# A decoder layer's input projection: eight block products against seven, and a new order of emission

## The chip, the cores and the metric

The kernel runs on one core of a Trainium2 chip. The metric is device time in microseconds (us); less is better. PE is the matmul engine, DVE the vector engine, ACT the activation engine, POOL the GpSimd engine, and SP the queue that issues the DMAs. Each engine works through its own instructions in the order in which the program emitted them, and an instruction that waits holds up all that stands behind it on its engine.

## What is computed

One layer over 2048 tokens of width 1024: a normalised input goes through one projection, its columns feed a gated delta-rule group (8 heads of 128) and a short gated convolution (8 groups of 128), and the two are mixed by an output projection.

```python
h = rmsnorm(x, norm_in_w)
proj = h @ w_in                       # 1024 x (8192 + 16) columns
qkv, z_g, b_g, a_g, gate_b, gate_c, h_c, z_c = split(proj)
qkv = silu(causal_depthwise_conv(qkv, conv_qkv_w))
...
o = gated_delta_rule_chunked(q, k, v, g, beta)     # state S carried from chunk to chunk
o = rmsnorm(o, gdn_norm_w) * silu(z_g)
y_c = gate_b * (causal_depthwise_conv(gate_c * h_c, conv_w) + conv_b) * silu(z_c)
out = rmsnorm(x + concat(o, y_c) @ w_out, final_norm_w)
```

## The kernel before

**Tiling.** The tokens are worked in two halves of 1024, each in two blocks of 512. The projection's columns are 64 tiles of 128, and one narrow tile for the gates. For each tile and block, `dense` (L449) makes one sum of products over the eight 128-row slices of the width. Operands are float32 split in two float16 parts, so each slice takes three matmuls of 512 columns (high by high, low by high, high by low): 24 for a tile and block, all on line L462. A weight tile is read anew in each half.

**Getting a weight tile ready.** `norm_w` (L376) sums the tile's squares on ACT (L383), reduces them over partitions by a small matmul (L386) and makes a power-of-two scale by a short chain over DVE and POOL (L138 to L141, L389, L390); it does so once for a column, in the first half. `split` (L408) makes the high part on ACT (L414) and the low part on DVE (L424).

**One head.** After its k, q and v tiles, `gdn` (L655) multiplies k by k and q (L706, `NA` on DVE at L710), sends the 32x32 diagonal blocks out by DMA, and `invert` (L869) inverts them on POOL by 60 instructions on 32 partitions (L876, L878). The inverses come back by DMA into `Wt`. DVE transposes them at L758, and the first small matmul that needs them is L767. Eight chunks follow, each a chain: L811 (state by k, PE), L812 (`r`, DVE), L817 (PE), L819 (`u`, ACT), L822 (PE), L826 (the state `S_all`, DVE). Matmuls of the dense tiles stand between its steps.

**What sets the order.** Every step is a generator that counts in slots; `slot` (L217) lets each that is due emit its next piece, and `dense` calls it after every eight matmuls. The plan of tiles and the constants at the head of the file (SHIFT, PACE, XL and others) were set by hand. Waits in a generator are numbers of slots.

**The output projection** (L1182 to L1184) is 1536 matmuls of 512 columns. `out_start` (L1085) loads the first weights and the first two mixed rows (`mr`, then `mm` by `split_mix`, L1024) while the last dense tiles are still running.

## Time and profile before

| | |
|---|---|
| median of 3 runs | 2199.77 us (2198.93 to 2204.18) |
| the profiled execution | 2200.84 us, of it 2199.0 us in the span that the profile shows |
| PE busy | 2088.5 us, 95% of the span |
| DVE, ACT, POOL busy | 1177.0, 747.4 and 788.7 us (54%, 34%, 36%) |
| mean granted PE clock | 0.974 of full speed |

Busy time is the share of the span in which an engine had an instruction running. PE's records overlap (a matmul's record is longer than the time to the next one), so its rate is read from the starts of matmuls that follow each other. Where an engine idles, the profile names the instruction that ended the idle time.

### The profile page before, as it was taken

To read this page: it belongs to the slowest core of one execution; us is meant where nothing else is said; L and a number is where in the kernel's file an instruction comes from. 1 tells how busy PE (TensorE), PEld (TensorE's weight loads), DVE (VectorE), ACT (ScalarE), POOL (GpSimd) and SP (SyncE) were. 2 spreads that over 40 slices of the span, in tenths; PEclk is the share of its full clock that TensorE was granted. 3 is DMA by queue.
4 is the path that set the end of the run, shared out by engine and by line. 5 is a ranking of instruction groups with operands and counts; after the bars stand their busy time and mean duration, and the time that the engine had idled before them with its cause. 6 is when DMAs were issued, how large, how long until landed. Compare 5 with 4: busy or idle time off the path is not lost.

```text
span 2199.0 us, 29850 instructions
## 1 busy us (share of the span) xinstructions
PE 2088.5 (95%) x11663; PEld 1252.0 (57%) x11663; DVE 1177.0 (54%) x2153; ACT 747.4 (34%) x1415; POOL 788.7 (36%) x1158
## 2 busy tenths in 40 slices
PE   5999999999999999899899998999899899999998
PEld 3445564645454545465456454555556456888886
DVE  4645566656555555567455455466456435224433
ACT  5524242525242424344224243232323123223221
POOL 2063526253535353605642536526262600000100
PEclk9999999999999999899999998999999999999999
DMA  4342223334653232333332233544434218334452
GB/s 118 59 72 47 70 58 72 54 75 51 77 55 72 48 80 51 116 59 72 49 73 62 64 59 65 46 80 68 53 67 67 64 39 277 125 115 153 162 173 87
DMA packets 235828, 178.98 MB, mean 81 GB/s; under 512 B 43677, under 2 KB 207910, under 8 KB 235686
## 3 DMA queue, kind: packets, MB, share of 16 engines
q1 hardware_dynamic: 235686, 177.06, 37.3%
q8 instruction: 92, 1.51, 0.3%
q14 instruction: 50, 0.41, 0.1%
HBM read 147.53 MB, written 29.49 MB: 81 GB/s over the span
## 4 chain that ended last, share of the span: by engine, by line
PE 62%; POOL 21%; DVE 6%; issue 5%; DMA 4%; ACT 1%; SPq 0%; POOLq 0%; DVEq 0%; ACTq 0%
PE ps_d L462 35%; POOL nb L878 9%; POOL nbt L876 8%; PE ps_d L1182 3%; PE ps_d L1184 3%; PE ps_r L1182 3%; PE ps_d L1183 3%; PE ps_r L1184 3%; PE ps_r L1183 3%; PE ps_t L706 2%; POOL oss L852 2%; DMA E<-gd 2%; PE ps_r L817 1%; PE ps_r L822 1%; DVE cacc L554 1%
## 5 line engine op out<-in xcount | busy, mean ns | idle before, releaser
L462 PE MATMUL ps_d<-hx,wh 128*128 128x512 f16 x4160 | 1284.7, 385 | 2.1 <-DVE hx L307 1.2
L462 PE MATMUL ps_d<-hx,wl 128*128 128x512 f16 x2048 | 789.0, 385 | 5.0 <-DVE craw L573 3.0
L462 PEld LDWEIGHTS <-wh 128*128 128x128 f16 x4160 | 411.9, 100 | 432.8 <-issue 27.1
L462 PEld LDWEIGHTS <-wl 128*128 128x128 f16 x2048 | 209.1, 102 | 220.1 <-issue 14.6
L876 POOL TENSOR_TENSOR nbt<-nb 32x30 f32<-32x30 f32 (+14 forms) x480 | 279.1, 581 | 121.7 <-DMA nb<-nd 88.0
L878 POOL TENSOR_TENSOR nb<-nb,nbt 32x30 f32<-32x30 f32 (+14 forms) x480 | 296.8, 618 | 37.6
L852 POOL TENSOR_TENSOR oss<-oss,nhalf_pow 128x16 f32<-128x16 f32 x32 | 102.2, 3195 | 268.7 <-DVE oss L851 255.4
L414 ACT ACTIVATE wh<-raw,wscale 128x1024 f16<-128x1024 f32 x130 | 148.7, 1144 | 141.3 <-DVE wscale L141 114.1
L554 DVE SCALAR_TENSOR_TENSOR cacc<-craw,cols_a,cacc 128x1024 f32<-128x1024 f32 x144 | 187.4, 1301 | 0.9
L424 DVE SCALAR_TENSOR_TENSOR wl<-raw,wscale,wh 128x1024 f16<-128x1024 f32 x128 | 172.8, 1350 | 19.3 <-ACT wh L414 18.9
L139 POOL TENSOR_TENSOR p<-p,nhalf_pow 128x1 f32<-128x1 f32 x66 | 36.0, 546 | 341.5 <-DVE p L138 341.5
L826 DVE SCALAR_TENSOR_TENSOR S_all<-S_all,dec,ps_r 128x128 f32<-128x128 f32 x120 | 41.5, 346 | 211.3 <-PE ps_r L822 211.3
L1072 POOL TENSOR_TENSOR stat<-stat,nhalf_pow 128x1 f32<-128x1 f32 x16 | 15.3, 957 | 353.5 <-DVE stat L1071 353.5
L577 ACT ACTIVATE craw<-ps_d,wscale 128x512 f32<-128x512 f32 x96 | 65.9, 686 | 200.1 <-PE ps_d L462 200.0
L1030 DVE TENSOR_TENSOR mm<-mr,mm 128x1024 fp32r<-128x1024 f32 x64 | 77.2, 1224 | 89.9 <-ACT mm L1028 89.9
L1182 PE MATMUL ps_d<-wo,mm 128*128 128x512 f32 x256 | 102.4, 400 | 0.1
L1182 PE MATMUL ps_r<-wo,mm 128*128 128x512 f32 x256 | 102.1, 399 | 0.0
L1184 PE MATMUL ps_d<-wo,mm 128*128 128x512 f32 x256 | 100.9, 394 | 0.0
L1184 PE MATMUL ps_r<-wo,mm 128*128 128x512 f32 x256 | 100.9, 394 | 0.0
L1183 PE MATMUL ps_d<-wo,mm 128*128 128x512 f32 x256 | 100.6, 393 | 0.1
L819 ACT ACTIVATE u<-ps_r 128x128 f32<-128x128 f32 x128 | 35.0, 273 | 193.4 <-PE ps_r L817 193.2
L1183 PE MATMUL ps_r<-wo,mm 128*128 128x512 f32 x256 | 100.4, 392 | 0.0
(228 smaller groups left out, 2628.8 us busy)
## 6 DMA issues: line engine op xcount, KB each, us to landing
raw<-in_w_in_dram SPq DMA_DIRECT2D x128, 512.0 KB, 8.0
mr<-mixd SPq DMA_DIRECT2D x64, 512.0 KB, 5.0
E<-gd SPq DMA_DIRECT2D x16, 512.0 KB, 9.3
qs<-gd SPq DMA_DIRECT2D x16, 512.0 KB, 4.2
mixd<-yy SPq DMA_DIRECT2D x16, 512.0 KB, 9.0
mixd<-zs SPq DMA_DIRECT2D x32, 256.0 KB, 2.6
wor<-in_w_out_dram SPq DMA_DIRECT2D x16, 512.0 KB, 5.6
x<-in_x_dram SPq DMA_DIRECT2D x8, 512.0 KB, 5.5
```

The source lines that it names most:

```text
L414: ACT.activation(wh, raw, AF.Copy, scale=s_)
L424: DVE.scalar_tensor_tensor(wl, raw, s_, wh, op0=ALU.mult, op1=ALU.subtract)
L462: PE.matmul(ps[:, 0:BLK], w_[:, k, :], x_[k, b], start=n == 0, stop=n == len(mm) - 1)
L554: DVE.scalar_tensor_tensor(acc, raw[:, j:j + HALF], wq(j, t), acc, op0=ALU.mult, op1=ALU.add)
L577: ACT.activation(raw[0][:, 3 + b * BLK:3 + (b + 1) * BLK], ps, AF.Copy, scale=inv)
L852: POOL.tensor_tensor(oss, oss, nhalf_pow[:, 0:1].to_broadcast([P, nq]), op=ALU.pow)
L876: POOL.tensor_tensor(tv, nb[:, 0:m, m:m + 1].to_broadcast([npart, m, n]), nb[:, m:m + 1, m + 1:32].to_broadcast([npart, m, n]), op=ALU.mult)
L878: POOL.tensor_tensor(nb[:, 0:m, m + 1:32], nb[:, 0:m, m + 1:32], tv, op=ALU.subtract)
L1030: DVE.tensor_tensor(mm[:, 1], mr, mm[:, 0], op=ALU.subtract)
L1182: PE.matmul(ps, mm[:, 0, kk, :], wh, start=k == 0, stop=False)
L1183: PE.matmul(ps, mm[:, 0, kk, :], wl, start=False, stop=False)
L1184: PE.matmul(ps, mm[:, 1, kk, :], wh, start=False, stop=k == KM - 1)
```

## The change

The weight tiles are taken in pairs (k with q, v with z, and the two pairs of the convolution). A pair's two tiles, cut into the two halves of the width, and the two token blocks of a half make a 2x2 by 2x2 product, done by one Strassen level in Winograd's form: seven block products of 4 slices for eight. Each product is 12 matmuls of 512 columns (`product`), so a pair takes 84 instead of 96. The gates' tile is not paired and has 80 matmuls in all instead of 64.

For this, `prepare` makes sums of weight blocks (`st`, `A21`, `A12`) and splits seven operands in float16 (tiles `g1` to `g4`, 3.5 tiles' worth a pair); the x blocks are made into seven operands too (`xop`). Those of the second half are made ahead, stored in DRAM (`x1d`) and loaded by `reload_x` when the first half no longer needs the buffers. Four of the products accumulate in one PSUM bank that ACT copies out four times (`chain`), the other three are added by DVE from banks of their own, with two sums of 512 columns between (`sums`); the products' scale is applied later. `either` gives some sums to POOL. The z gate goes through DRAM (`zd`).

The order of emission comes from clocks: `Clock` keeps an estimated time for each engine and for each tile's readiness, with costs written into the code, and `do` emits an instruction when its inputs are ready by these clocks within 0.3 us and its engine's clock is at most 1.2 us (or `back`) ahead of PE's. The matmuls of the projection are emitted two at a time between rounds of all generators. The loads for the output projection and its first splits are spawned after the last product.

```diff
-SHIFT = (0, 3, 5)
-PACE = 1.75
-XL = (3, 3)
-PAIR = (1,0)
-END = (0,1)
-WS = 4
-NG = (2, 2)
-TG = 2
-WBEG = 2
+BACK = 1.2
+PEQ, DRAIN, SEM = 0.43, 0.2, 0.06
...
+    def cost(self, eng, op, outs, ins, a, k):
...
+        if eng == "POOL":
+            if k.get("op") == ALU.pow:
+                return 0.45 + 0.185 * n
+            if op == "tensor_tensor":
+                return 0.2 + 0.0026 * n
+            return 0.2 + 0.0012 * n
...
-    def slot():
-        clock[0] += 1
-        for t in list(tasks):
-            if t[0] <= clock[0]:
-                try:
-                    t[0] = clock[0] + next(t[1])
-                except StopIteration:
-                    tasks.remove(t)
-
...
+    def do(fn, *a, back=BACK, lead=0.3, **k):
+        e = fn.eng
+        while True:
+            t = clk.ready(e, a, k)
+            cur, q = now(), clk.t[e]
+            late = t > max(cur, q) + lead
+            if not late and q <= cur + back:
+                break
+            yield max(t - lead if late else 0.0, q - back, cur + 0.02)
+        fn(*a, **k)
...
+    def either(n=512):
+        return POOL if max(now(), clk.t["POOL"]) + 0.2 + 0.0026 * n <= \
+            max(now(), clk.t["DVE"]) + 1.0 + 0.001 * n else DVE
...
-            scales[cols[i][0]] = s_, inv
-            ss = sm.tile([P, 1], F32, tag="wss", name="wss")
-            junk = hp.tile([P, KD * P], mybir.dt.bfloat16, tag="r7", name="junk")
-            ACT.activation(junk, raws[i].rearrange("p k c -> p (k c)"), AF.Square, accum_out=ss)
-            yield 3
-            pt = ps_t()
-            PE.matmul(pt[:, 0:1], ones, ss, start=True, stop=True)
-            pow2_below(s_, pt[:, 0:1], 8192.0)
-            yield 1
-            DVE.reciprocal(inv, s_)
...
-            ACT.activation(wh, raw, AF.Copy, scale=s_)
...
-                DVE.scalar_tensor_tensor(wl, raw, s_, wh, op0=ALU.mult, op1=ALU.subtract)
...
+    def reload_x():
+        yield from need(("x1d",))
+        for o in PRODUCTS:
+            yield from need(("free", o))
+            xop[o] = hp.tile([P, KT, 2, BLK], F16, tag=f"X{o}", name="xop")
+            yield from do(SP.dma_start, xop[o].rearrange("p k s w -> p (k s w)"), x1d[o])
+            for kt in range(KT):
+                mark("x1", o, kt)
...
+            yield from do(ACT.activation, g1[:, 0], r1, AF.Copy, scale=s1)
+            st = wst.tile([P, 2, KT, P], F32, tag="st", name="st")
+            A11, A12, A21, A22 = r1[:, 0:KT], r1[:, KT:KD], r2[:, 0:KT], r2[:, KT:KD]
+            yield from do(DVE.scalar_tensor_tensor, g1[:, 1], r1, s1, g1[:, 0],
+                          op0=ALU.mult, op1=ALU.subtract)
+            yield from do(DVE.scalar_tensor_tensor, st[:, 1], A21, rho, A11,
+                          op0=ALU.mult, op1=ALU.subtract)
+            yield from do(either().tensor_tensor, A21, A21, A22, op=ALU.add)
+            yield from do(DVE.scalar_tensor_tensor, st[:, 0], A21, rho, A11,
+                          op0=ALU.mult, op1=ALU.subtract)
+            g2 = wst.tile([P, 2, 2, KT, P], F16, tag="G2", name="g2", bufs=2)
+            yield from do(ACT.activation, g2[:, 0], st, AF.Copy, scale=s1)
+            yield from do(either().tensor_tensor, A12, A12, st[:, 0], op=ALU.subtract)
+            yield from do(DVE.scalar_tensor_tensor, g2[:, 1], st, s1, g2[:, 0],
+                          op0=ALU.mult, op1=ALU.subtract)
+            g4 = wst.tile([P, 2, KT, P], F16, tag="G4", name="g4", bufs=1)
+            yield from do(ACT.activation, g4[:, 0], A12, AF.Copy, scale=s1)
+            yield from do(DVE.scalar_tensor_tensor, g4[:, 1], A12, s1, g4[:, 0],
+                          op0=ALU.mult, op1=ALU.subtract)
+            g3 = wst.tile([P, 2, KD, P], F16, tag="G3", name="g3", bufs=1)
+            yield from do(ACT.activation, g3[:, 0], r2, AF.Copy, scale=s2)
+            yield from do(DVE.scalar_tensor_tensor, g3[:, 1], r2, s2, g3[:, 0],
+                          op0=ALU.mult, op1=ALU.subtract)
...
-        for k in range(KD):
-            mm += [(wh, k, xh), (wh, k, xl)] + ([(wl, k, xh)] if wl is not None else [])
-        for n, (w_, k, x_) in enumerate(mm):
-            while (k, b) not in xh:
-                slot()
-            PE.matmul(ps[:, 0:BLK], w_[:, k, :], x_[k, b], start=n == 0, stop=n == len(mm) - 1)
-            if n % 8 == 7 and n + 1 < len(mm):
-                slot()
-        if fr:
...
+    def product(ps, p, half, j, start, stop=True):
+        o = PRODUCTS[j]
+        wait_for(("w", p, {0: 0, 1: 0, 2: 2, 6: 2, 3: 3, 4: 4, 5: 4}[j]))
+        w = ops.pop((p, j))
+        tag = "x1" if half else "x"
+        for kt in range(KT):
+            wait_for((tag, o, kt))
+            for a, b in ((0, 0), (0, 1), (1, 0)):
+                mm(ps, w(kt, a), xop[o][:, kt, b], start=start and kt == 0 and a + b == 0,
+                   stop=stop and kt == KT - 1 and a == 1,
+                   skip_group_check=not j % 2)
+        run()
...
+        def chain(y):
+            yield from need((p, 0))
+            yield from do(ACT.activation, p1, y, AF.Copy, back=9.0)
...
+        def sums(d):
+            yield from need((p, 1))
+            yield from do(DVE.tensor_tensor, p1, d[1], p1, op=ALU.add, back=9.0)
+            yield from need((p, "y4"))
+            yield from do(either().tensor_tensor, u2, u2, u4, op=ALU.subtract, back=9.0)
+            yield from do(DVE.tensor_tensor, u4, d[3], u4, op=ALU.add, back=9.0)
+            yield from need((p, "y6"))
+            yield from do(either().tensor_tensor, u2, u2, o2[:, BLK:], op=ALU.add, back=9.0)
+            yield from do(DVE.tensor_tensor, u2, d[5], u2, op=ALU.add, back=9.0)
...
+    def out_start():
+        yield from need(*[("post", 2 * H - 1, b) for b in range(2)], *[("mixc", 1, g) for g in range(G)])
+        spawn(load_mix(), 1)
+        spawn(split_mix(), 1)
...
+    mark("quads")
+    spawn(load_wo(), 1)
+    spawn(split_wo(), 1)
+    spawn(load_res(), 2)
+    spawn(load_fnw(), 2)
+    spawn(out_start(), 1)
```

On PE, the chain of one chunk among the projection's matmuls, from the state's matmul (`ps_r<-S_all,kq`) on. Before, from the middle of the first half:

```order
L811 MATMUL ps_r<-S_all,kq 128x128
L814 MATMUL po<-qs,S_all 128x128
L462 LDWEIGHTS wh
L462 MATMUL ps_d<-hx,wh 128x512
L462 LDWEIGHTS wl
L462 MATMUL ps_d<-hx,wl 128x512
L462 LDWEIGHTS wh
L462 MATMUL ps_d<-hx,wh 128x512
L462 LDWEIGHTS wh
L462 MATMUL ps_d<-hx,wh 128x512
L462 LDWEIGHTS wl
L462 MATMUL ps_d<-hx,wl 128x512
```

Three more dense matmuls stand behind these before the chain's next step, so there are eight. Now, the same place of a chunk in the first half (all instructions of the engines have the line L183, the recording wrapper):

```order
L183 MATMUL ps_r<-S_all,kq 128x128
L183 MATMUL ps_o<-kq,S_all 128x128
L183 LDWEIGHTS g_2266
L183 MATMUL ps_d<-xop,g_2266 128x512
L183 LDWEIGHTS g_2266
L183 MATMUL ps_d<-xop,g_2266 128x512
L183 MATMUL ps_r<-r,Wt_164 128x128
L183 LDWEIGHTS g_2266
L183 MATMUL ps_d<-xop,g_2266 128x512
L183 LDWEIGHTS g_2266
L183 MATMUL ps_d<-xop,g_2266 128x512
L183 MATMUL ps_r<-u,kst 128x128
```

Two matmuls stand now where eight stood, at each step of the chain.

On DVE, a stretch of the second half in which dense tiles run beside a head's work. Before:

```order
L424 SCALAR_TENSOR_TENSOR wl<-raw,wscale,wh 128x1024
L738 TENSOR_REDUCE qss<-vp 128x32
L861 SCALAR_TENSOR_TENSOR zs<-on,cols_b,zs 128x512
L748 TENSOR_TENSOR vp<-ps_t,rn 128x512
L843 STREAM_TRANSPOSE on<-osq 128x512
L845 TENSOR_REDUCE op<-on 128x16
L846 SCALAR_TENSOR_TENSOR op<-qss,op 128x16
L748 TENSOR_TENSOR vp<-ps_t,rn 128x512
L752 TENSOR_TENSOR qs<-qs,kq 128x1024
L851 TENSOR_SCALAR oss<-ps_t 128x16
L967 TENSOR_TENSOR yy<-yy,zc 128x1024
L424 SCALAR_TENSOR_TENSOR wl<-raw,wscale,wh 128x1024
```

Now (`g` and `st` are weight operands, `c` the projection's results, `raw` the weights):

```order
L183 SCALAR_TENSOR_TENSOR g_9906<-raw,wsc,g_9906 128x1024
L183 SCALAR_TENSOR_TENSOR st<-raw,wsc 128x512
L183 TENSOR_TENSOR oc<-oc,osq 128x512
L183 SCALAR_TENSOR_TENSOR zb<-oc,cols_b,zb 128x512
L183 SCALAR_TENSOR_TENSOR vacc<-c_9450,wq,vacc 128x1024
L183 SCALAR_TENSOR_TENSOR st<-raw,wsc 128x512
L183 TENSOR_TENSOR raw<-raw,st 128x512
L183 TENSOR_TENSOR c_9812<-c_9812,c_9811 128x512
L183 TENSOR_TENSOR c_9811<-ps_d,c_9811 128x512
L183 STREAM_TRANSPOSE on<-osq 128x512
L183 SCALAR_TENSOR_TENSOR g_9973<-st,wsc,g_9973 128x1024
L183 SCALAR_TENSOR_TENSOR g_10003<-raw,wsc,g_10003 128x512
```

Between a head's own instructions stand now several of the weights' preparation and of the results' sums, most of them with two inputs in SBUF, where one `wl` stood.

On SP's queue, the passage from the projection to the output projection (`wor` are its weights, `mr` the mixed rows, `res` and `xo` the residual, `mixd<-yy` or `mixd<-c` a finished convolution group). Before:

```order
L405 DMA raw<-in_w_in_dram 128x8x128 x3
L969 DMA mixd<-yy 128x8x128
L995 DMA wor<-in_w_out_dram 128x2x512 x2
L1021 DMA mr<-mixd 128x1024 x4
L864 DMA mixd<-zs 128x4x128
L1021 DMA mr<-mixd 128x1024 x2
L995 DMA wor<-in_w_out_dram 128x2x512 x4
L1054 DMA res<-in_x_dram 128x512 x2
L1021 DMA mr<-mixd 128x1024
```

Now:

```order
L183 DMA mixd<-zb 128x4x128
L183 DMA wor<-in_w_out_dram 128x2x512 x3
L183 DMA res<-in_x_dram 128x512 x16
L183 DMA xo<-in_x_dram 128x512 x4
L183 DMA fnw<-in_final_norm_w_dram 128x1024
L183 DMA wor<-in_w_out_dram 128x2x512 x3
L183 DMA mixd<-c_15325 128x8x128
L183 DMA mr<-mixd 128x1024
L183 DMA wor<-in_w_out_dram 128x2x512 x3
L183 DMA mr<-mixd 128x1024 x5
```

The first load of mixed rows stood right behind the first weights; it stands now behind all residual loads and behind the last group's store.

## Rows read from the trace of the kernel before

**Rows 1.** The page's head and part 1: busy time, share of the span, instructions.

```profile
span 2199.0 us, 29850 instructions
PE 2088.5 (95%) x11663; PEld 1252.0 (57%) x11663; DVE 1177.0 (54%) x2153; ACT 747.4 (34%) x1415; POOL 788.7 (36%) x1158
```

**Rows 2.** Windows: stretch, then busy us of each engine, granted clock, DMA share, GB/s.

```profile
0.00:27.30 27.30, 8.41 (x43) 7.24 (x44) 14.81 (x40) 15.58 (x25) 8.81 (x26) 0.92 0.72 211
27.30:1820.00 1792.70, 1708.69 (x10030) 951.46 (x10031) 1013.57 (x1916) 628.45 (x1230) 761.67 (x1115) 0.97 0.35 64
1820.00:2199.00 379.00, 371.41 (x1593) 293.33 (x1591) 148.63 (x198) 103.41 (x162) 18.20 (x17) 0.99 0.46 155
```

**Rows 3.** Chain that ended last, one piece: start, length, engine, line, count.

```profile
359.15 10.38 PE ps_d L462 x48
```

**Rows 4.** Groups by line on PE: count, then busy us, mean ns of one.

```profile
L462 PE MATMUL ps_d<-hx,wh 128*128 128x512 f16 x4160 | 1284.7, 385 | 2.1 <-DVE hx L307 1.2 <-ACT hx L306 0.8
L462 PE MATMUL ps_d<-hx,wl 128*128 128x512 f16 x2048 | 789.0, 385 | 5.0 <-DVE craw L573 3.0 <-DVE wl L424 2.0
```

**Rows 5.** Groups by line and form on DVE and ACT, columns as in Rows 4.

```profile
L424 DVE SCALAR_TENSOR_TENSOR wl<-raw,wscale,wh 128x1024 f16<-128x1024 f32 x128 | 172.8, 1350 | 19.3 <-ACT wh L414 18.9
L1060 DVE TENSOR_TENSOR res<-ps_d,res 128x512 f32<-128x512 f32 x8 | 5.5, 689 | 20.2 <-PE ps_d L1184 20.2
L1076 DVE SCALAR_TENSOR_TENSOR res<-res,stat,fnw 128x512 f32<-128x512 f32 x16 | 12.0, 750 | 4.4 <-POOL stat L1072 4.4
L414 ACT ACTIVATE wh<-raw,wscale 128x1024 f16<-128x1024 f32 x130 | 148.7, 1144 | 141.3 <-DVE wscale L141 114.1 <-PE ps_d L462 21.4 <-DMA mixd<-zs 5.6
L1011 ACT ACTIVATE wo<-wor 128x512 fp32r<-128x512 f32 x32 | 18.9, 622 | 21.9 <-PE ps_r L1184 18.2 <-DMA wor<-in_w_out_dram 3.8
```

**Rows 6.** Windows over three heads' inversions on POOL, columns as in Rows 2.

```profile
429.40:471.70 42.30, 39.25 (x189) 19.35 (x188) 24.63 (x44) 10.68 (x16) 37.91 (x65) 0.96 0.25 49
1014.40:1065.90 51.50, 49.47 (x235) 24.41 (x233) 38.91 (x45) 19.79 (x41) 46.89 (x62) 1.00 0.30 66
1080.10:1116.90 36.80, 36.80 (x218) 21.77 (x217) 10.17 (x18) 7.88 (x14) 32.12 (x61) 1.00 0.22 58
```

**Rows 7.** Timeline of POOL in the second of them: start, us, instruction.

```profile
1020.78 0.50 POOL L878 TENSOR_TENSOR nb<-nb,nbt 32x168 f32<-32x168 f32 x1
...
1024.98 1.50 POOL L878 TENSOR_TENSOR nb<-nb,nbt 32x198 f32<-32x198 f32 x1
```

**Rows 8.** Timeline of DVE, ahead of that inversion and in it.

```profile
1008.97 1.28 DVE L424 SCALAR_TENSOR_TENSOR wl<-raw,wscale,wh 128x1024 f16<-128x1024 f32 x1
...
1022.89 1.58 DVE L424 SCALAR_TENSOR_TENSOR wl<-raw,wscale,wh 128x1024 f16<-128x1024 f32 x1
```

**Rows 9.** Waits of PE: who, for whom, us in total, times, longest.

```profile
PE ps_t L767 <- DVE Vt L758: 27.9, 8, 5.6
PE ps_r L822 <- ACT u L819: 1.6, 3, 0.7
```

**Rows 10.** Timeline of all engines at one step of a chain.

```profile
1809.49 0.38 PE L817 MATMUL ps_r<-r,Wt 128*128 128x128 f32 x2
1809.70 0.69 ACT L650 ACTIVATE zs<-ps_d,wscale 128x512 f32<-128x512 f32 x1 [5.43 <-PE ps_d L462]
1810.28 0.27 ACT L819 ACTIVATE u<-ps_r 128x128 f32<-128x128 f32 x1
...
1810.60 0.49 PE L822 MATMUL ps_r<-u,kst 128*128 128x128 f32 x2 [0.72 <-ACT u L819]
```

**Rows 11.** Timeline of ACT at the start: the first weights' squares, the first result's evacuation.

```profile
13.51 1.06 ACT L383 ACTIVATE junk<-raw 128x1024 bf16<-128x1024 f32 x1 [2.11 <-DMA raw<-in_w_in_dram]
...
34.00 0.69 ACT L577 ACTIVATE craw<-ps_d,wscale 128x512 f32<-128x512 f32 x1 [0.28 <-PE ps_d L462]
```

**Rows 12.** DMA issues: KB each, median us from issue to landing.

```profile
mr<-mixd SPq DMA_DIRECT2D x64, 512.0 KB, 5.0
...
mixd<-yy SPq DMA_DIRECT2D x16, 512.0 KB, 9.0
```

1886 lines of the change are left out of this document (1047 added, 839 removed).

## The prediction, made before the change was run

> **What bounds the kernel now.** The page comes first: PE is busy for 2088.5 of 2199.0 us, the other engines for 34 to 54% [rows 1]. Busy PE alone proves little, since its records overlap, so the second view is the windows by stage. The start up to the first dense matmul takes 27.3 us. The projection with the heads' work in it takes 1792.7 us, and PE is busy for 1708.7 of them, so 84 us are idle. The output projection takes 379.0 us with PE busy for 371.4 [rows 2]. Third, the rate: in the chain that ended last, 48 dense matmuls take 10.38 us, which is 0.2163 us each, with nothing between them [rows 3]. The 4160 and 2048 matmuls of L462 [rows 4] at this rate are 1343 us, three quarters of the middle stage. PE's longest waits are for the inverted blocks that DVE transposes, 28 us in 8 waits, and the chain's steps cost next to nothing: 1.6 us at L822 [rows 9]. So the kernel is bound by PE's work. Every matmul taken away is time, as long as nothing else becomes late.
>
> The profiled execution took 2200.84 us, 1.84 more than its span and 1.07 more than the median. The sum is made against it, and 1 us is taken off at the end.
>
> **What is removed.** The 6208 dense matmuls become 64 pairs x 7 products x 12, and 80 for the gates: 5456. That is 752 fewer, at 0.2163 us: -162.7 us [rows 3, 4]. Their shape stays 128x512 and each still brings its own weight load, so I take the rate as it is. 33 tiny matmuls of the scales go too; they are left out. The output projection keeps its 1536 matmuls.
>
> **What DVE and ACT get for it.** A pair cost DVE two low parts, 2 x 1.35 us [rows 5]. Now it has three splits of the same size (4.05), one of half (0.75), two weight sums at 0.75, three additions from PSUM at 0.69 (2.07), and of four more sums about 1.7 on DVE (107 of them in the order, at 0.69: 1.15): 9.5 us [rows 5]. Over 64 pairs that is 608 against 173 us, so +435 us. In the middle stage DVE was busy for 1013.6 us [rows 2]; it will be for some 1450 of about 1700 us, 85%. ACT also grows, by four evacuations and 3.5 splits a pair, but it starts at 628 of 1793 us [rows 2] and stays well below DVE. DVE's 435 us lie beside PE's work, so by themselves they cost nothing. What they do to the instructions that PE waits for is the next two terms.
>
> **The inversion on POOL.** A head's inverse is made by 60 POOL instructions. Three windows over whole inversions show what DVE does to them. With DVE busy for 10.17 of 36.8 us the inversion takes 36.8 us, with 24.63 of 42.3 it takes 42.3, with 38.91 of 51.5 it takes 51.5 [rows 6]. Inside the last, a subtraction of 168 elements takes 0.50 us while DVE is on other work, and one of 198 takes 1.50 us beside DVE's two-input instructions [rows 7]. DVE pays less: the same split takes 1.28 us ahead of the inversion and 1.58 us in it [rows 8]. From 58% to 76% of DVE is 9.2 us, so at 85% I estimate 56 us, 14 above the usual 42. By the order, one to five of the new sums of 128x512 (three on average) fall in an inversion on POOL as well; at 0.50 x 512/168 = 1.5 us each I count 5 us. So the inverse comes some 20 us later (14 + 5) after the head's own products. PE's order leaves no more room for it than before: between the last product of k and q and the first use of the inverse stand 230 dense matmuls on average, where 229 stood, and before they were just short of enough (28 us of waits in all [rows 9]).
>
> Not all of the 20 us is lost. DVE stands too once it reaches the transposes, and then POOL goes on at the pace of the 36.8 us window: 17 of the 20 us after PE's own delays become 11. PE's further waits in that stretch, of which the next term is one, use up about half. I take 5.5 us for each of 16 heads, 88 us, less the 28 of before: **+60 us**. The ends are -28 (the order happens to fit everywhere) and +180 (13 a head).
>
> **The chain.** Eight dense matmuls stood between a chain's steps; now the commonest number between L817 and L822 is two (67 of 128), so 0.22 us of the step itself and 0.43 of dense work. The row shows 1.11 us from one start to the other, when ACT had to finish another evacuation first (it ended at 1810.39 and `u` started at 1810.28, so part of it was ACT's) [rows 10]. Of 128 such steps 102 stand closer than 1.11 us; what is short adds up to 37 us, and 20 us for the two steps through DVE. With 0.85 us as the price when ACT is free it would be some 20 us in all. I take **+30 us**, nearer to the lower end since ACT stays half idle.
>
> **The start.** ACT finished nothing of the first tile before 34.0 us [rows 11], and the first product here needs no more than that. But the third product needs x blocks that are made from both token blocks. By the order, ACT has 21 splits and copies of 128x512 at 0.62 us, 6 scaled evacuations at 0.69 and 7 instructions on weights (about 1.1 each) to do between the first evacuation and the third product's, 25 us [rows 5, 11], while PE has some 15 us of work. Against the old start, which also idled, that is **+18 us** (10 to 30).
>
> **The passage to the output projection.** Before, the mixed rows were loaded while dense tiles still ran. Now the last group is stored after the last product's sums, its silu and its product (about 5 us by the rows of such instructions); the store lands in 9.0 us, the load behind it in 5.0 [rows 12], and ACT and DVE split it. The first load needs only the heads' part, so it need not wait for the store to land, but it stands behind 21 loads on SP's queue. I take **+22 us** (14 to 30, the upper end with everything in series).
>
> **What the new order gives back.** PE's 84 idle us of before [rows 2] held more than the 28 above: waits at places where a number of slots was too short. An order by readiness should lose less there; I take **-20 us** (0 to -40).
>
> **The sum.** 2200.8 - 162.7 + 60 + 30 + 18 + 22 - 20 = 2148; less 1 for the median, 2147 us, 2.4% faster.
>
> **The rivals.**
> *The order absorbs it (2072 us).* If the clocks' costs are right for POOL under load, the inverse comes when PE gets to it. Then the first term is nothing, the chain 20, the start 15 and the passage 18: 2200.8 - 162.7 + 20 + 15 + 18 - 20 = 2071. For it speaks that the cost in the code, 0.2 + 0.0026 n us, adds up to 38 us for an inversion, near the time at DVE's old load. Against it: DVE's load is no longer the old one [rows 6].
> *POOL starves behind DVE (2245 us, slower).* The mechanism is that of rows 7, with its place at the transposes ahead of the first use of the inverse. If nearly every POOL instruction there waits out a DVE instruction, as 1.50 for 0.50 us shows [rows 7], 60 of them take 80 us or more; PE then waits 11 us or more a head, 180 in all or 150 more than before, and the chain's end through DVE goes to 45: 2200.8 - 162.7 + 150 + 45 + 18 + 22 - 20 = 2253, some 2245 if the start is at its lower end. It decides from about 9 us a head: there the gain is gone. The Trainium skill (SBUF — State Buffer, "Who interferes with whom") says of this that a DVE instruction with two SBUF inputs and a GpSimd instruction that reads SBUF exclude each other, the later one fully blocked. By that rule both would be serial wherever both have work, and this rival would be the forecast. The trace agrees for POOL (1.50 for 0.50 us) but shows DVE held for only 0.3 us of 1.28 [rows 7, 8].
> *It does less than it says (about 2200 us).* With the terms at their middle and 3 us a head more on the inversion's path (48 us) the sum is 2195, within 0.3% of before: the matmuls go, and the same time comes back as waits of PE.
>
> **How the numbers follow.** Forecast's neighbourhood (2100 to 2190): 0.48. Absorbed, below 2100: 0.24. About the same: 0.06. Starved: 0.22. A measurement of this kernel can tell about 0.3%, some 7 us. So faster 0.72, same 0.06, slower 0.22. The range is 2068 to 2245: it takes in the first rival's value and the second's, and leaves about 2 in 10 outside.
>
> **What would show it.** L183's matmuls on `xop` must number 5376 and 80, at 0.216 us when dense. In the middle stage DVE should be busy for 80 to 90% and PE idle for 150 to 250 us. Waits of PE for `Vt` (DVE) near 90 us confirm the inversion's term, near 0 or above 200 the rivals; an inversion should last some 50 to 60 us. Waits for `u`, `r` and `S_all` should add up to 20 to 50 us. PE should stand still for about 20 us ahead of the first `wo` matmul. I am wrong if DVE is idle in much of the middle stage while PE waits for something else, such as the weights' operands or x blocks that come back from DRAM at the half's change.

## The result: 20% slower, and the profile of the changed kernel

The changed kernel takes 2644.95 us (median of 4 runs, 2640.95 to 2648.69), the kernel before 2200.41 on the same chip: a ratio of 1.2017 (95% interval 1.199 to 1.2043). The forecast was 2147 us, at most 2245.

The head of the changed kernel's page and its part 1, which answer to [rows 1]:

```profile
span 2645.9 us, 29590 instructions
PE 2121.5 (80%) x10847; PEld 1238.5 (47%) x10847; DVE 1710.7 (65%) x2669; ACT 996.4 (38%) x1764; POOL 1179.7 (45%) x1283
```

The windows by stage, columns as in [rows 2]: the start, the projection with the heads, the passage, the output projection:

```profile
0.00:29.90 29.90, 6.98 (x24) 4.39 (x25) 13.31 (x43) 16.21 (x28) 10.12 (x26) 1.00 0.74 198
29.90:2187.00 2157.10, 1726.63 (x9287) 933.01 (x9288) 1551.24 (x2434) 876.32 (x1575) 1152.43 (x1240) 0.88 0.40 68
2187.00:2209.00 22.00, 0.42 (x3) 0.02 (x1) 11.06 (x15) 9.36 (x15) 2.69 (x1) 0.59 1.05 385
2209.00:2645.90 436.90, 387.48 (x1536) 301.08 (x1536) 135.13 (x180) 94.53 (x147) 14.50 (x16) 0.93 0.34 112
```

These rows hold the whole account. Behind the start, PE was busy for 1708.69 + 371.41 = 2080.1 us before [rows 2] and is now for 1726.63 + 0.42 + 387.48 = 2114.5: 34 us more, although the dense matmuls that are gone were 163 us of work. So the work that is left takes 197 us longer; the granted clock of the middle stage fell from 0.97 to 0.88. As an estimate, PE's busy time in windows of 2 us, each times what its clock lacked of full speed, adds up to 45 us before and 195 now, so the clock makes some 150 of the 197 us; the rest was not taken apart. PE stands still for 430.5 + 21.6 + 49.4 = 501.5 us, where it was 84.0 + 7.6 = 91.6: 410 us more. With 2.6 us at the start, 197 - 163 + 410 + 3 is the 447 us by which the span grew.

PE's waits in the changed kernel: for whom, us in total, times, the longest ([rows 9] showed 27.9 for Vt and 1.6 for u):

```profile
PE ps_t L183 <- ACT junk_sq L183: 160.7, 25, 23.8
PE ps_t L183 <- DVE Vt L183: 71.6, 10, 10.8
PE ps_y L183 <- ACT c L183: 42.9, 13, 7.0
PE ps_d L183 <- ACT mm L183: 40.2, 9, 21.6
PE ps_t L183 <- DVE op L183: 31.8, 19, 6.5
PE ps_r L183 <- DVE S_all L183: 29.5, 19, 5.0
PE ps_t L183 <- DMA Wt<-wd: 14.0, 2, 7.8
...
PE ps_y L183 <- ACT xop L183: 12.2, 2, 7.7
...
PE ps_r L183 <- DVE r L183: 8.5, 8, 4.9
...
PE ps_r L183 <- ACT u L183: 3.6, 3, 3.0
PE ps_d L183 <- DVE xop L183: 3.1, 2, 1.6
PE ps_y L183 <- DVE xop L183: 2.3, 4, 1.1
```

The largest is one that the prediction doesn't have: the small matmul that sums a weight tile's squares for its scale. It stands in PE's queue until the tile has landed and ACT has squared it, and the products behind it stand too. Below it come the inverse (Vt and Wt, 85.6 us, near the forecast's 90) and a field of smaller waits for DVE and ACT.

### The profile page after: what moved, and what is told of

Read it like the earlier page. It is cut to its first block, busy times and chain, and to the rows that moved or that the text cites. A ratio compares the mean times of both kernels' runs of the same rounds, so it can differ in the third digit from the quotient of the medians.

```text
span 2645.9 us, 29590 instructions
## 1 busy us (share of the span) xinstructions
PE 2121.5 (80%) x10847; PEld 1238.5 (47%) x10847; DVE 1710.7 (65%) x2669; ACT 996.4 (38%) x1764; POOL 1179.7 (45%) x1283
## 5 line engine op out<-in xcount | busy, mean ns | idle before, releaser
L183 PEld LDWEIGHTS <-g 128*128 128x128 f16 x5376 | 547.8, 103 | 675.1 <-issue 169.1
L183 PE MATMUL ps_y<-xop,g 128*128 128x512 f16 x3072 | 803.3, 403 | 73.1 <-ACT c L183 42.9
L183 PE MATMUL ps_d<-xop,g 128*128 128x512 f16 x2304 | 589.5, 396 | 9.0 <-DVE c L183 5.7
L183 POOL TENSOR_TENSOR nbt<-nb 32x30 f32<-32x30 f32 (+14 forms) x480 | 373.1, 777 | 104.9 <-DMA nb<-nd 70.8
L183 POOL TENSOR_TENSOR nb<-nb,nbt 32x30 f32<-32x30 f32 (+14 forms) x480 | 372.4, 776 | 34.5
L183 ACT ACTIVATE c<-ps_y 128x512 f32<-128x512 f32 x256 | 150.8, 590 | 299.9 <-PE ps_y L183 299.1
L183 DVE SCALAR_TENSOR_TENSOR g<-raw,wsc,g 128x1024 f16<-128x1024 f32 (+1 forms) x192 | 235.9, 1237 | 14.0 <-ACT g L183 12.9
L183 ACT ACTIVATE g<-raw,wsc 128x1024 f16<-128x1024 f32 (+1 forms) x192 | 189.8, 1000 | 114.3 <-PE ps_d L183 68.5
L183 PE MATMUL ps_d<-wo,mm 128*128 128x512 f32 x768 | 195.2, 413 | 46.6 <-ACT mm L183 40.2
L183 PE MATMUL ps_y<-wo,mm 128*128 128x512 f32 x768 | 194.8, 414 | 17.3 <-ACT mm L183 13.6
L183 POOL TENSOR_TENSOR stat<-stat,nhalf_pow 128x1 f32<-128x1 f32 x16 | 14.5, 920 | 433.2 <-DVE stat L183 433.2
L183 PEld LDWEIGHTS ps_d<-wo,mm 128*128 128x128 f32 x768 | 150.0, 197 | 90.6 <-ACT mm L183 44.2
L183 ACT ACTIVATE mm<-mr 128x1024 fp32r<-128x1024 f32 x64 | 65.9, 1051 | 307.2 <-issue 147.7
L183 PEld LDWEIGHTS ps_y<-wo,mm 128*128 128x128 f32 x768 | 151.1, 198 | 59.7 <-ACT mm L183 16.7
L183 DVE TENSOR_TENSOR mm<-mr,mm 128x1024 fp32r<-128x1024 f32 x64 | 77.4, 1221 | 152.4 <-ACT mm L183 152.4
L183 DVE SCALAR_TENSOR_TENSOR st<-raw,wsc 128x512 f32<-128x512 f32 x128 | 110.7, 865 | 69.3 <-POOL raw L183 59.2
L183 DVE TENSOR_TENSOR c<-ps_d,c 128x512 f32<-128x512 f32 x192 | 131.5, 685 | 34.8 <-POOL c L183 20.4
L183 POOL TENSOR_TENSOR raw<-raw 128x512 f32<-128x512 f32 x61 | 82.2, 1348 | 148.8 <-DVE st L183 72.4
L183 PE MATMUL ps_t<-wss,ones 128*128 128x2 f32 (+1 forms) x66 | 16.3, 317 | 162.6 <-ACT junk_sq L183 160.7
L183 DVE SCALAR_TENSOR_TENSOR kq<-c,wq,kq 128x1024 f32<-128x1024 f32 x96 | 136.1, 1421 | 3.3 <-ACT kq L183 2.1
L183 POOL TENSOR_TENSOR oss<-oss,nhalf_pow 128x16 f32<-128x16 f32 x32 | 105.9, 3308 | 63.8 <-DVE oss L183 63.8
L183 ACT ACTIVATE g<-st,wsc 128x1024 f16<-128x1024 f32 x64 | 73.4, 1147 | 161.3 <-DVE st L183 161.2
```

The lines of the kernel that those rows point to most:

```text
L183: return raw(*a, **k)
```

## Is it the order? Experiments in the changed kernel

Two theories stood at first. **A**: the new order is planned with times that are too short, so PE's queue holds instructions whose operands come late. **B**: DVE and POOL have too much to do for what hangs on them, in any order.

**The scale taken out of PE's queue.** In the edits, `plan_only` keeps an instruction in the clocks, so that the order stays, but doesn't issue it.

```diff
-                    yield from do(ACT.activation, junk_sq, r..., AF.Square, accum_out=ss[:, j:j + 1])
+                    yield from plan_only(ACT.activation, junk_sq, r..., AF.Square, accum_out=ss[:, j:j + 1])
-                yield from do(PE.matmul, pt[:, 0:2], ones, ss, start=True, stop=True)
+                yield from plan_only(PE.matmul, pt[:, 0:2], ones, ss, start=True, stop=True)
```

> The changed kernel with all instructions in their places, but without the weights' squares on ACT and without the small matmuls on PE that sum them over partitions (64 and 32 of them, first half); the scales are a constant. So PE no longer stands at a small matmul until a weight tile has landed and been squared. Theory A (the order was made with too short times; PE's queue is held at the scale's matmul while the products behind it could run): the 160.7 us of waits for junk_sq vanish and do not come back elsewhere, and of the dense matmuls at the lower clock some 30 us go with them: 2440 to 2490 us. Theory B (the weights are late by themselves, since DVE and the loads cannot keep up, and the small matmul is only the first place that shows it): the waits come back ahead of the products as waits for g, and the time stays above 2560 us.

2585.44 us: 60 us less, of the 155 to 205 that theory A wanted. The waits for `junk_sq` are gone, and others grew instead, as PE's waits in this kernel show:

```profile
PE ps_t L183 <- DVE Vt L183: 115.3, 18, 24.9
PE ps_y L183 <- ACT c L183: 56.9, 17, 9.6
PE ps_t L183 <- DVE op L183: 46.2, 19, 13.3
...
PE ps_r L183 <- DVE S_all L183: 38.5, 22, 7.6
```

Vt rose by 44 us, the other three by 14, 14 and 9. What PE doesn't lose at the scale it mostly loses later, at the heads' work and not, as theory B had it, at the weights' operands `g` (7 us more).

**The order planned anew with measured times.** First the DMAs' landing, then POOL's and DVE's times as well:

```diff
-            done = self.dma + 0.6
+            done = self.dma + 0.6 + 2.4 * n * size / 200e3
```

> One constant of the clocks changed: a DMA counts as landed later, by 2.4 times its own transfer time (a 512 KB weight tile about 11 us after its issue, where the clocks counted 4.5 and the trace shows 10.0); and the tile qss has three buffers for two. The order of all engines is planned anew from that. Theory A (the order was made with too short times, and the loads' is the worst): waits for junk_sq fall below 60 us and the time to 2400 to 2520 us. Theory B (the loads and DVE cannot keep up in any order): the waits move to the products, the time stays above 2580 us. The same matmuls and sums are done in both cases.

2613.65 us; waits for `junk_sq` fell to 36.1 us, those for Vt rose to 94.9 and two new ones came, for the weights' operands `g` (63.3 and 28.3 us).

```diff
-                return 0.2 + 0.0026 * n
+                if o.shape[0] == 32:
+                    return 0.25 + 0.0032 * n
+                return 0.18 + 0.00235 * n
...
+            return d * 1.12 if n >= 256 and not ps and op != "tensor_reduce" else d
```

> The changed kernel with more of the clocks' costs set by the trace: DMAs as in e4, POOL's instructions on 32 partitions 0.25 + 0.0032 n us (the trace: 0.78 us in the mean, counted 0.63), DVE's large instructions between SBUF tiles 12% longer, its reductions by what they read (1.21 us for 128x1024, counted 0.21). The order is planned anew. Theory A in what e4 left of it (the order was made with too short times, for POOL and DVE too): 2450 to 2550 us. Theory B (DVE and POOL have too much to do for what hangs on them, in any order): above 2570 us, since e4 already gave back only 31 of 445 us.

2650.58 us, no better than the changed kernel. Theory A has fallen as far as the planner's times go: with DMA times near the measured ones this planner's order gains 31 us, with the others corrected too nothing. That no other order would be faster is not shown.

**What DVE and POOL carry.** Two runs take load off and leave the order alone.

```diff
+            put = do if m % 8 == 0 else plan_only
-            yield from do(POOL.tensor_tensor, tv, ..., op=ALU.mult)
+            yield from put(POOL.tensor_tensor, tv, ..., op=ALU.mult)
```

> The changed kernel with all instructions in their places, but with 6 of the 60 POOL instructions of each inversion (the others are left out, so the blocks are not inverted). The prediction's term for the inversion was 88 us of PE's waits, and the trace shows 71.6 (Vt) and 14.0 (Wt). If that term is right, these waits vanish, some 25 us of matmuls at the lower clock with them, and the time falls to 2520 to 2560 us. If the inverse was not what PE waited for last there (DVE's work ahead of the transposes, or the DMAs), less than 40 us go: above 2600 us.

2508.19 us, 137 less: more than the waits for Vt and Wt, of which 61 remain. The middle stage's row shows a second gain:

```profile
29.70:2048.40 2018.70, 1690.62 (x9288) 917.65 (x9288) 1460.97 (x2434) 878.50 (x1575) 510.47 (x376) 0.90 0.43 73
```

With most of the inversions' instructions gone from POOL, the same 2434 instructions keep DVE busy for 1460.97 us instead of 1551.24. So POOL's work lengthens DVE's as well, and the 137 us are not the price of the inverse alone.

```diff
-            yield from do(DVE.scalar_tensor_tensor, g1[:, 1], r1, s1, g1[:, 0], ...)
+            yield from plan_only(DVE.scalar_tensor_tensor, g1[:, 1], r1, s1, g1[:, 0], ...)
+            nc.vector.scalar_tensor_tensor(g1[:, 1, 0], r1[:, 0], s1, g1[:, 0, 0], ...)
```

(The other three low parts of a pair are cut down in the same way.)

> The changed kernel with all instructions in their places, but each of DVE's 256 low parts of weights does an eighth of its columns (a quarter for the two with 512), and the products read that part again and again, so the results are not the projection's. PE's and ACT's work is the same, DVE has some 250 us less to do. Theory B (PE waits for instructions that stand in DVE's queue behind these): the waits for Vt, S_all, op and c fall to about half, and the time to 2450 to 2540 us. If DVE, at 74% in the middle, is not what holds PE (the DMAs, ACT and PE's own order are): above 2600 us.

2536.59 us, 108 less. DVE was busy for 217 us less in the middle stage, so each us of DVE was worth 0.50. The time is the one of theory B; PE's waits for Vt, `S_all`, `op` and `c` fell from 176 to 127 us, by a quarter and not by half. The edits of e1, e2 and e7 together:

> e1 (no sums of squares ahead of the scales), e2 (6 of 60 POOL instructions in an inversion) and e7 (an eighth of DVE's low parts) together, in the changed kernel's order. If each takes away a cause of its own, 60 and 137 us and e7's gain add up: below 2350 us. If PE's waits have one cause that moves from place to place (theory B: the weights' and the heads' work compete for the same DVE and POOL, and the place where PE stands is chance), the gains of e2 and e7 overlap and the time stays above 2400 us. In both cases the dense matmuls run at the higher clock for more of the time, a granted clock of 0.93 or more.

2369.19 us: 276 less, where 60 + 137 + 108 is 305. Between the two bounds of the expectation: the gains nearly add up, so they are mostly causes of their own. But the kernel is still 7.7% slower than before.

**The output projection.** This one has a cause of its own:

```diff
-        for j in range(len(jobs)):
-            for h in range(2):
+    by_pair = [(j + i, h) for j in range(0, len(jobs), 2) for h in range(2) for i in range(2)]
+        for j, h in by_pair:
```

> The changed kernel with the loads and splits of the mixed rows in another order: of each pair of token tiles that PE works on together, first both tiles' first halves, then both second halves (before: a tile's two halves, then the other tile's). PE waits for mm at every pair, 42 us in all, because ACT's split of the second tile's first half stands behind a split that has to wait for the pair's end. If that order is the cause, the output projection goes from 436.9 to 375 to 395 us with its slow matmuls, and the time to 2585 to 2605 us. If the loads of the mixed rows are too slow (16 x 4 of 512 KB), it stays above 420 us and the time above 2630 us.

2583.69 us, 61 less, and the stage's row (as above) is now near that of before, whose first output matmul comes at 1832 us, so that the stage takes 367 us of the span of 2199.0 (the third window of [rows 2] begins 12 us earlier, among the last dense matmuls):

```profile
2202.40:2576.30 373.90, 362.58 (x1536) 289.21 (x1536) 135.19 (x180) 94.54 (x147) 8.59 (x16) 0.98 0.39 131
```

**PE's clock.** Three windows of the changed kernel: 20 us in which PE waits for a scale, the matmuls right behind, and a stretch without waits (columns as in [rows 2]; the third number from the end is the granted clock):

```profile
764.00:784.10 20.10, 0.00 (x0) 0.00 (x0) 13.02 (x12) 6.23 (x10) 15.54 (x14) 0.50 0.55 46
784.10:789.50 5.40, 5.36 (x34) 2.50 (x35) 3.43 (x11) 3.39 (x5) 1.15 (x1) 0.63 0.60 46
1500.00:1526.00 26.00, 26.00 (x122) 11.84 (x121) 21.07 (x24) 9.71 (x12) 24.20 (x26) 1.00 0.43 82
```

The clock goes to 0.50, the lower of its two levels (1.2 GHz), while PE stands, and is still low for part of the work behind. Whether the standing is the cause, a run with work in the place of waits tells:

```diff
+                for _ in range(FILL.get(p, 0)):
+                    nc.tensor.matmul(pt, xop[X11][:, 0, 0, 0:P], xop[X11][:, 0, 0], start=True, stop=True)
                 yield from do(PE.matmul, pt[:, 0:2], ones, ss, start=True, stop=True)
```

> The changed kernel with 665 matmuls of 128x512 added on PE, whose results nothing reads. They stand ahead of 22 of the scales' matmuls, at each about as many as PE waited there in the trace (wait less 0.4 us, by 0.2163 us). If PE's lower clock comes from its standing still (granted clock 0.888 against 0.974 before), PE now works where it stood, so the waits for junk_sq shrink to less than 40 us, the granted clock rises to 0.90 or more and the time falls by the some 30 to 45 us of slow matmuls that follow these waits: 2595 to 2620 us. If the clock has another cause, the added work can only cost: 2645 us or more.

2602.22 us: 665 matmuls more, and 43 us less. The row of its middle stage with the passage:

```profile
29.70:2165.00 2135.30, 1831.89 (x9953) 983.30 (x9953) 1561.29 (x2448) 886.14 (x1590) 1167.70 (x1241) 0.91 0.42 73
```

The clock is 0.91 for 0.88. PE is busy for 105 us more than in the changed kernel (1726.63 + 0.42), where 665 matmuls at 0.2163 us make 144: by this estimate the other matmuls take 39 us less. So a wait of PE is paid a second time, in part, by slow matmuls behind it. The Trainium skill ("TensorE: Matmul & The Clock Gate", "HAM oscillation — how this bites in real kernels") describes such a PE, which falls back to the lower clock at each wait between short bursts; the trace agrees (0.50 in the wait above, 0.63 behind it).

## Is it the load? Experiments in the kernel before

The decisive runs leave the new kernel alone. They put parts of the change into the old kernel with its hand-set order. First the saving alone, then DVE's load alone, then both edits together:

```diff
+        step = 8 if wl is None else 7
+        mm = mm[:16 if wl is None else 21]
...
-            if n % 8 == 7 and n + 1 < len(mm):
+            if n % step == step - 1 and n + 1 < len(mm):
```

> The kernel before, in its own hand-set order, with 21 of the 24 matmuls of each tile and block (768 fewer; the last three, of the last slice, are left out, so the projection is incomplete), seven between two slots for eight. It is the change's saving on PE without anything that it adds. If the saving holds as the prediction counted it (768 x 0.2163 = 166 us), less some 6 us a head by which the room ahead of the inverse shrinks (200 matmuls for 229; up to 100 us): 2070 to 2135 us. If PE was only just the bound and the heads' work takes its place, the time stays above 2150 us.

```diff
-                DVE.scalar_tensor_tensor(wl, raw, s_, wh, op0=ALU.mult, op1=ALU.subtract)
+                for _ in range(4):
+                    DVE.scalar_tensor_tensor(wl, raw, s_, wh, op0=ALU.mult, op1=ALU.subtract)
```

> The kernel before, complete, but each weight tile's low part (128x1024 on DVE, 1.35 us) is computed four times over: 384 instructions and some 530 us of DVE more, as much as DVE has more to do in the middle of the changed kernel (1551 for 1014 us). Same order, nothing else changed. Theory B (DVE's load makes the inversion and PE's other waits long): the inversions take 55 to 60 us for 44, PE waits some 13 us more a head, 2350 us or more. If the hand-set order has room for it, below 2280 us; then it is not the load alone that makes the changed kernel slow but its order with that load.

> e10 and e11 together: the kernel before in its hand-set order with 768 matmuls fewer and DVE's load of the changed kernel. This is the sum of the prediction (2147 us, 2068 to 2245) without the new order of emission and without what the change adds on ACT and POOL. If the prediction's terms were right and the new order lost the rest: 2080 to 2250 us. If the load alone makes the changed kernel slow (theory B): above 2400 us.

They took 2150.31, 2567.19 and 2557.27 us (before beside them: 2201.02). The row of the projection's stage, from the first product to the first of the output projection, in before and then in these three:

```profile
27.30:1831.80 1804.50, 1720.49 (x10085) 956.78 (x10086) 1020.57 (x1926) 633.20 (x1236) 764.56 (x1116) 0.97 0.36 65
```

```profile
27.90:1782.90 1755.00, 1595.81 (x9317) 894.21 (x9318) 1024.52 (x1926) 632.50 (x1236) 772.16 (x1116) 0.94 0.46 67
```

```profile
31.30:2201.00 2169.70, 1824.01 (x10086) 981.72 (x10086) 1527.00 (x2307) 629.45 (x1230) 893.61 (x1117) 0.93 0.30 54
```

```profile
31.40:2182.20 2150.80, 1707.03 (x9317) 926.17 (x9318) 1526.84 (x2305) 628.88 (x1230) 891.48 (x1117) 0.89 0.38 54
```

Three readings. 768 matmuls are 166 us of work, but taking them out brings 50 (at the edge of what the expectation gave to the heads' work, above 2150 us): PE's busy time falls by 125 only, at a lower clock, and its idle time grows from 84 to 159. DVE's load alone costs 366 us, with every matmul as it was: PE's idle time grows to 346, and its busy time by 104. And once that load is there, the matmuls' saving is worth 10 us. The last run has neither Strassen's sums nor the new order, yet at 2557 it stands 88 us from the changed kernel; the 61 us of the output projection's order and the 22 of the passage would be nearly all of that. Theory B's bounds (2350 and 2400 us) hold in both. But that the two times lie so near is partly chance, since PE waits at other places. In e12 it waits longest for the chain's `r`, for which it waits 8.5 us in the changed kernel:

```profile
PE ps_r L820 <- DVE r L815: 81.7, 29, 6.0
```

So the runs show that the load is enough to make the old order this slow, not that the changed kernel loses the same microseconds. The added work also stands in lumps, four subtractions in a row for each weight tile, 5 to 6 us long; the changed kernel's are 0.7 to 1.4 us each and stand among others (the order on DVE ahead of the prediction). The price of a us of DVE there is e7's 0.50.

**By which way does DVE reach PE?** B1: DVE's two-input instructions (both inputs in SBUF) hold up POOL's inversion. B2: the heads' own DVE instructions stand in DVE's queue behind the added ones. One run shuts the first way, one the second:

```diff
+                for _ in range(3):
+                    sums = sm.tile([P, KD], F32, tag="sums", name="sums")
+                    DVE.tensor_reduce(sums, raw, axis=mybir.AxisListType.X, op=ALU.add)
```

> The kernel before, complete, with three more instructions on DVE for each weight tile, as e11, but of another kind: reductions of 128x1024 with one input in SBUF (1.21 us by such a row of before, 465 us in all), where e11 had subtractions with two (518 us). Two ways lead from DVE's load to PE: B1, two-input instructions hold up POOL's inversion (in e11 it took 52.6 us for 43.8); B2, the heads' own DVE instructions (r, S_all, op, transposes) stand in DVE's queue behind the added ones. B1: the inversions stay at 43 to 46 us and the time below 2290 us. B2: the inversions stay there too, but the time is 2450 to 2550 us, nearly that of e11 (2567).

```diff
-            POOL.tensor_tensor(tv, ..., op=ALU.mult)
+            for _ in range(2 if 10 <= m <= 21 else 1):
+                POOL.tensor_tensor(tv, ..., op=ALU.mult)
```

> The kernel before, complete, with DVE's load as it was, but 12 of the 30 multiplications of each inversion on POOL issued twice, which makes it some 9 us longer, as DVE's load did in e11. B1: PE waits some 9 us more at each of the 16 heads, 2330 to 2400 us with the matmuls at the lower clock that follow. B2 (the inverse is a small part of e11's 367 us): below 2270 us.

2405.28 and 2331.90 us (before beside them: 2196.52), 209 and 135 more. e14 gave the number of B1, e13 lies between those of B1 and B2: both ways are open. The same head's inversion as the last of [rows 6] (36.80 us with 10.17 of DVE), in e11, e13 and e14:

```profile
1304.40:1354.10 49.70, 46.45 (x267) 26.69 (x266) 31.86 (x39) 8.16 (x15) 45.07 (x62) 1.00 0.16 43
```

```profile
1201.00:1238.00 37.00, 37.00 (x218) 21.80 (x217) 20.14 (x27) 7.89 (x14) 32.38 (x61) 1.00 0.22 56
```

```profile
1168.50:1214.50 46.00, 45.57 (x256) 26.89 (x256) 15.04 (x27) 8.44 (x16) 40.40 (x74) 1.00 0.18 46
```

With reductions DVE is twice as busy as before and the inversion doesn't lengthen; with subtractions it takes 13 us more. In the mean of the 16 heads, read from POOL's timelines, the inversion takes 43.8 us before, 52.6, 44.6 and 53.3 in these three. So e13 is the way over the queue alone: 414 us of DVE cost 209, 0.50 each. PE's waits in before, and the largest in e13, show where:

```profile
PE ps_r L817 <- DVE r L812: 5.0, 5, 2.6
...
PE ps_r L811 <- DVE S_all L826: 3.3, 3, 2.0
```

```profile
PE ps_r L820 <- DVE r L815: 54.3, 30, 4.4
PE ps_t L770 <- DVE Vt L761: 33.0, 13, 6.6
PE ps_r L814 <- DVE S_all L829: 25.6, 17, 3.0
```

It is the chain's two steps through DVE that grow; Vt had 27.9 us [rows 9]. e14 is the way over POOL: 9.5 us a head cost 135, 8.5 a head. Not all of that is the inverse. PE's waits for Vt grow from 27.9 to 67.6 us, but DVE also waits 206.0 us, where it waited 141.3, for the scales' small powers (L139), which stand in POOL's queue too. The two together are 344 us, or 391 with e13 scaled to e11's 507 us of DVE; e11 measured 366. The Trainium skill ("SBUF — State Buffer", "Who interferes with whom") says that a DVE instruction with two SBUF inputs contends with a GpSimd instruction that reads SBUF and a reduction never does. The runs agree, down to the reductions' own times (shortest, median, longest of 384, in ns):

```profile
L427 DVE TENSOR_REDUCE sums<-raw x384: 1198/1208/1216, 24.2 to 2017.1; 128x8 f32<-128x1024 f32 x192
```

The way over the queue looks like this in e11's timeline of DVE, and then of PE:

```profile
274.99 6.01 DVE L425 SCALAR_TENSOR_TENSOR wl<-raw,wscale,wh 128x1024 f16<-128x1024 f32 x4
280.92 0.34 DVE L813 SCALAR_TENSOR_TENSOR r<-ps_r,dec,vp 128x128 f32<-128x128 f32 x1
```

```profile
281.32 0.58 PE L818 MATMUL ps_r<-r,Wt 128*128 128x128 f32 x1 [5.61 <-DVE r L813]
```

A 0.34 us step of a chain stands behind 6 us of weights, and PE stands for 5.61.

**Was before already there?** Less and more load:

```diff
-                DVE.scalar_tensor_tensor(wl, raw, s_, wh, op0=ALU.mult, op1=ALU.subtract)
+                DVE.scalar_tensor_tensor(wl[:, 0], raw[:, 0], s_, wh[:, 0], op0=ALU.mult, op1=ALU.subtract)
```

> The kernel before with an eighth of each weight tile's low part on DVE (some 140 us of DVE less; PE multiplies by that eighth again and again, so the projection is not the reference's). PE's work is the same. If before is bound by PE's work with DVE hidden, as the prediction had it, nothing happens: 2190 to 2210 us. If the heads' work on DVE and POOL bounds it together with PE (theory B), some of the 84 us of waits and 37 us of slow matmuls go: 2110 to 2180 us.

```diff
-                DVE.scalar_tensor_tensor(wl, raw, s_, wh, op0=ALU.mult, op1=ALU.subtract)
+                for _ in range(2):
+                    DVE.scalar_tensor_tensor(wl, raw, s_, wh, op0=ALU.mult, op1=ALU.subtract)
```

> The kernel before, complete, with each weight tile's low part computed twice (e11: four times), some 175 us of DVE more. If DVE's load is paid for from the first microsecond (the price of e11, 367 us for 518, is 0.71 us for each): 2300 to 2340 us. If there is room that only the larger load uses up: below 2250 us.

2139.33 and 2262.63 us, the first as theory B had it, the second less than the full price and more than none. DVE's busy time in the stage was 903 and 1190 us (before 1021), so 117 us less brought 57 (0.49 each) and 169 more cost 66 (0.39). In this range DVE's load is never hidden: before stood on the slope already, with PE 95% busy. In e11 the price is 0.72; whether that comes of the larger load or of the longer lump (four subtractions in a row for two) is not shown.

## Two runs that follow from these

**Sums on POOL.** In the changed kernel there is a third way, seen in one timeline of all engines:

```profile
1941.02 1.25 POOL L183 TENSOR_TENSOR raw<-raw 128x512 f32<-128x512 f32 x1
1942.24 0.59 POOL L183 TENSOR_TENSOR nb<-nb,nbt 32x220 f32<-32x220 f32 x1
1942.31 1.08 DVE L183 SCALAR_TENSOR_TENSOR st<-raw,wsc 128x512 f32<-128x512 f32 x1 [4.69 <-POOL raw L183]
...
1944.31 0.33 DVE L183 SCALAR_TENSOR_TENSOR S_all<-S_all,dec,ps_r 128x128 f32<-128x128 f32 x1
...
1944.70 0.58 PE L183 MATMUL ps_r<-S_all,kq 128*128 128x128 f32 x1 [4.97 <-DVE S_all L183]
```

A sum of weights was given to POOL in the midst of an inversion; DVE waits 4.69 us for it with `S_all` behind, and PE waits 4.97 us for `S_all`. The run gives these sums to DVE, at the same places:

```diff
-        return POOL if max(now(), clk.t["POOL"]) + ...
+        return Moved if max(now(), clk.t["POOL"]) + ...    # planned as POOL's, issued on DVE
```

> The changed kernel with the sums that it gave to POOL (some 165, of weights and results, 1.35 to 1.5 us each there) done by DVE at the same places of the order (about 0.7 us each, 115 us in all). They hold POOL's inversions up (6.6 us a head), and DVE and POOL wait for each other through them (DVE st for POOL raw 59 us; S_all and r stand behind). By the prices of e14 (135 us for 9.5 us a head) and e7 (109 us for 217 us of DVE): 58 us more for DVE's load, 94 us less for the inversions. If the two engines' waits for each other matter: 2560 to 2620 us. If DVE's load outweighs them: 2660 us or more.

2605.21 us, 40 less. That is what the two prices gave (58 - 94 = -36), but not for their reason. The middle stage's row in this run:

```profile
29.40:2139.10 2109.70, 1721.96 (x9288) 926.52 (x9288) 1588.59 (x2594) 876.27 (x1575) 950.68 (x1080) 0.88 0.41 70
```

DVE is busy for 37 us more, not 115, and an inversion is only 2.6 us shorter in the mean, not 6.6. By the same prices that is 19 - 37, some 18 us less. PE's waits fell from 29.5 to 19.7 us for `S_all` and from 42.9 to 25.7 for `c`, which fits the third way, but no run shows that way by itself.

**A complete kernel that follows from e15.** If DVE's time is paid for in the old kernel, saving some must make it faster:

```diff
+            kept = not ba and i >= ncol0
+            if kept:
+                wl = wst.tile([P, KD, P], F16, tag="wl", name="wl")
+                SP.dma_start(wl, wld[wld_at[col]])
...
+            if not ba and not kept:
+                yield 2
+                SP.dma_start(wld[wld_at.setdefault(col, len(wld_at))], wl)
```

> A complete kernel that follows from e15: the kernel before, with the low parts of the weights stored to DRAM in the first half (64 stores of 256 KB) and loaded from there in the second, where DVE computed them again. DVE has 64 x 1.35 = 86 us less to do in the second half; PE's work, the order and everything else stay. By e15's price (57 us for 141 us of DVE, 0.40 each) some 35 us: 2155 to 2185 us, with the inversions of the second half at 39 to 42 us. If the loads land after PE wants them (they are issued one tile, some 10 us, ahead on SP's queue and behind what waits there), PE waits for wl: 2200 us or more.

2171.22 us against 2196.67 beside it: a ratio of 0.9875 (95% interval 0.9853 to 0.9898). Its projection stage, as above:

```profile
27.30:1803.20 1775.90, 1712.61 (x10085) 952.69 (x10086) 943.00 (x1862) 632.47 (x1236) 738.43 (x1116) 0.98 0.43 86
```

DVE has 78 us less, PE's idle time falls from 84 to 63 us, and 25 us are gained, 0.33 for each us of DVE.

## Why the prediction was wrong, step by step

- **What bounds the kernel: this step failed.** "So the kernel is bound by PE's work. Every matmul taken away is time" was read from PE's 95% and 84 idle us. e10 shows 50 us for 166 us of matmuls, e15 57 us for 117 us of DVE. The signs to look for gave PE 150 to 250 us of idle time in the middle stage; it had 430.5. A small idle time says only that the hand-set order had balanced PE against the heads' work on DVE and POOL; it doesn't say that one of them has room.
- **DVE's load "by themselves they cost nothing": this step failed worst.** The load was sized 435 us and measured 538 (1551.24 against 1013.57 [rows 2]). The sizing went by times of before, but instructions grew longer (a weight sum took 0.87 us for 0.75), and e2 shows that some 90 us of DVE's time come from POOL's inversions beside it. The two terms for what it does were 60 + 30; in the old order the load alone, at 507 us, costs 366 (e11), and at the changed kernel's own price (e7, 0.50) 538 us come to some 270. The sum had no bound for it from above: all of the 435 us on PE's path would have been 2147 - 90 + 435 = 2492, far outside the range, and nothing in the rows excluded half of that.
- **The inversion: length right, price too low.** Forecast were some 61 us (56 + 5) for an inversion; the mean of 16 is 60.0. PE's waits for it are 85.6 us, forecast 88. But the sum let 20 us of delay a head cost 5.5; e14 shows 8.5 for 9.5 us, with what POOL holds up besides the inverse and with the slow matmuls.
- **The chain: right in its waits, wrong in its limits.** `S_all`, `r` and `u` hold PE for 29.5 + 8.5 + 3.6 = 42 us, 32 more than the 10 of before; forecast +30. The step looked at ACT and at the distance in matmuls. The steps that DVE's queue lengthens most are the chain's own, `r` and `S_all` (e13), and in the changed kernel it also holds up `op` and the transposes.
- **PE's clock: left out.** The sum took the dense rate "as it is"; the work that is left took 197 us longer, some 150 of it by the clock (estimate above). [rows 2] had 0.97 in it, the waits that were forecast had no clock beside them.
- **The scales: left out by a sentence.** "33 tiny matmuls of the scales go too; they are left out": those that stay hold PE for 160.7 us. Taken away, they give 60; the rest only moves (e1).
- **"What the new order gives back", -20: wrong in sign.** PE waits at more places than before, and better costs give 31 us of that back (e4) or nothing (e5).
- **The passage: right.** 22 us forecast, 22.00 measured, and by the forecast's way: on SP's queue the first load of mixed rows stands behind the residual loads and the last group's store, and is issued at 2198.58 us, some 11 us after the last product. **The output projection** was taken as unchanged, but lost 70 us (436.9 for 367), 61 of them by an order of splits that stands in the code (e6). The prediction's 379.0 us for it are 12 too many, for the reason given at e6.
- **The start: right.** The first product comes 2.6 us later, and PE waits some 18 us for the x operands (`xop`) behind it, all within the first 100 us: 20 us in all, forecast 18.
- **The matmuls' count: right.** 3072 + 2304 + 80 = 5456.
- **The rivals.** "POOL starves behind DVE" had the mechanism and the sign, at 2245 us and a chance of 0.22; it priced the way over POOL, gave the chain through DVE's queue 45 us, and left out the clock.

Open is what keeps e9 at 2369 us, 170 above before, with 163 us of matmuls gone and more than half of DVE's added load as well. The output order accounts for 61 of it. PE still stands 219 us in its middle stage, most for Vt (80.8 us); this was not taken apart. Open is also what the new order costs by itself: no run has it with the old eight products and without the load.

## What to carry to other kernels

A tuned kernel whose main engine is 95% busy can be in balance with a second engine at 54%: here work taken from the first brought a third of its time, and work added to the second cost 0.4 to 0.7 of its own, long before it was full. So before moving work to an engine "with room", ask which short steps of a chain stand in its queue, and measure the price with one run that issues an instruction of that engine twice (e16). And count a wait of PE for more than its own time: the slow matmuls behind 410 us of waits took some 150 us more.
